# Turning eight tiles in one out-of-place transpose in a fused LoRA kernel

## The chip, the core and the metric

The kernel runs on one core of a Trainium2 chip. The metric is the device time of one execution in microseconds. The kernel before took 124.73 us in the median of three runs (124.68 to 125.21). Engines are named as in the profile: PE is TensorE (matmul), PEld its weight loads, DVE is VectorE, ACT is ScalarE, POOL is GpSimd, SP is SyncE, which here issues all transfers on one queue.

## The reference

A low-rank correction is added to an activation tensor:

```python
batch, seq, d_model, r = 16, 512, 768, 16
lora = np.matmul(np.matmul(x, A), B)      # x: 8192 x 768, A: 768 x 16, B: 16 x 768
return (x + scale * lora).astype(np.float32)   # scale = 0.5
```

All tensors are float32 in memory. x and the output are 25.2 MB each; A and B are 48 KB each.

## The kernel before

The 8,192 rows of x are 64 tiles of 128 rows. They come in five parts of 8, 8, 16, 16 and 16 tiles (`PARTS`), by seven loads: load 0 (2 tiles), load 1 (6), load 2 (8), load 3 (16), load 4 (16), loads 5 and 6 (8 each). `x_sb` has room for 48 tiles; the last 16 take the place of the first 16. SP issues the loads 0 to 4 at the start, then store 0 when group 0 is summed, store 1 when group 1 is summed, load 5 when store 0 has landed, load 6 when store 1 has landed, and then the stores 2 (16 tiles, groups 2 and 3), 3 (16 tiles, groups 4 and 5), 4 and 5 (8 tiles each, groups 6 and 7). The result is added in place, so each store goes out of the same tiles.

The computation works on eight groups of eight tiles (`GROUP`), and each group goes through six steps:

1. **Narrowing** (`narrowed`): four tiles at a time are cast to float16, the first half of a group by ACT, the second by POOL (in group 0 both by ACT). It writes `xh0` or `xh1`.
2. **Turning** (`turned`): DVE transposes blocks of 32 x 32 of the half group in place, with two float16 values read as one float32 value.
3. **Projecting** (`projected`): 24 matmuls of 128 columns per half group, with a block-diagonal form of A (`w_bd`) as weights, sum y = x A into `ps_yt`. This PSUM tile holds both halves.
4. **Spreading**: four ACT instructions (L222) scale y and write it block-diagonally into `y_bd`.
5. **Raising** (`raised`): for each pair of tiles four matmuls with `b_mm` (B, repeated) write y B into one of two PSUM buffers `lora_ps`.
6. **Summing** (`summed`): DVE adds the PSUM buffer to the pair in `x_sb`. There are four pairs in a group.

The order of work on each engine is written out by hand, and semaphores join the engines. DVE does, for each half of a group, the turn of that half of the next group and then the two adds of this group. PE runs a hardware loop over the eight groups. A round raises two pairs of the group before, projects the first half of this group, raises the other two pairs, and projects the second half; the first round raises from a `y_bd` that still holds zeros, and four raises follow the loop. Narrowing a half waits until the projection of that half one group earlier has read the buffer (L175, on `s_y`). ACT narrows the first half of the next group and then spreads this group (L217 to L223). `raised` waits on `s_free` for its PSUM buffer; where a store follows group g, the last of these is given by SP (L137).

At the start POOL builds the weights `w_bd` from A, whose transpose is a DVE instruction at L227, PE repeats B over the partitions by two matmuls (L292), and ACT casts that into `b_mm` (L214).

The two orders in the code:

```python
        for g in range(NG):                 # DVE, L248
            for h in range(2):
                if g + 1 < NG:
                    turned(g + 1, h)
                summed(g, 2 * h)
                summed(g, 2 * h + 1)
```

Of the kernel before, what the change touches and what calls it, by code (L numbers as in the profile page):

```python
# [9 lines left out]
MM_DT = mybir.dt.float16  # L10
# [6 lines left out]
GROUP = 8  # L17

SUB = 4

APART = 8
# [3 lines left out]
def kernel(  # L25
# [25 lines left out]
    def sb(name, shape, dtype):  # L51
        return nc.alloc_sbuf_tensor(name, shape, dtype).ap()
# [15 lines left out]
    pick = sb("pick", [P, NQ, Q], MM_DT)  # L68
    w_bd = sb("w_bd", [P, NC, 2, P], MM_DT)
    b_mm = sb("b_mm", [P, D], MM_DT)  # L70
    xh = [sb(f"xh{h}", [P, SUB, D], MM_DT) for h in range(2)]
    y_bd = sb("y_bd", [P, GROUP, P], MM_DT)
    lora = [ps(f"lora_ps{i}", [P, 2, D]) for i in range(2)]
    y_ps = ps("ps_yt", [P, GROUP, Q])
# [32 lines left out]
    s_a, s_b = sem("s_a"), sem("s_b")  # L107
    s_ready, s_brows, s_pick = sem("s_ready"), sem("s_brows"), sem("s_pick")
    s_w, s_bh, s_bp, s_bm = sem("s_w"), sem("s_bh"), sem("s_bp"), sem("s_bm")
    s_narrow = [sem(f"s_narrow{h}") for h in range(2)]  # L110
    s_y, s_spread = sem("s_y"), sem("s_spread")
    s_turned = [sem(f"s_turned{h}") for h in range(2)]
    s_lora = sem("s_lora")

    s_free = [sem(f"s_free{p}") for p in range(PAIRS)]
    s_sum = sem("s_sum")
# [10 lines left out]
    def on_sync(e):  # L127
        def load(k):
            ld = LOADS[k]
            e.dma_start(out=held(*ld), in_=memory(x2, *ld)).then_inc(s_load[k], 16)  # L130

        def store(k, done):
            st = STORES[k]
            e.wait_ge(s_sum, k + 1)
            if STORED[k] + 1 < NG:

                e.sem_inc(s_free[PAIRS - 1], 1)  # L137
            e.dma_start(out=memory(out2, *st), in_=held(*st)).then_inc(done, 16)

        load(0)  # L140
        load(1)
        e.wait_ge(s_ready, 1)
        e.dma_start(
            out=a_rows[0 : NC * APART : APART, :], in_=A.rearrange("(c e) r -> c (e r)", e=64)
        ).then_inc(s_a, 16)
        e.wait_ge(s_brows, 1)
        e.dma_start(out=b_rows[0 : R * APART : APART, :], in_=B).then_inc(s_b, 16)
        for k in range(2, len(LOADS) - 2):
            load(k)

        e.sem_inc(s_spread, 1)
        for p, n in ((0, 1), (2, 2), (3, 2)):
            e.sem_inc(s_free[p], n)

        e.wait_ge(s_lora, 1)
        e.sem_inc(s_free[1], 1)
        store(0, s_out0)
        store(1, s_out1)
        e.wait_ge(s_out0, 16)
        load(len(LOADS) - 2)  # L160
        e.wait_ge(s_out1, 16)
        load(len(LOADS) - 1)
        for k in range(2, len(STORES)):
            store(k, s_out)

    here = set()

    def narrowed(e, copy, g, h):
        t = g * GROUP + h * SUB
        for k in dict.fromkeys(load_of(t + k) for k in range(SUB)):  # L170
            if (e, k) not in here:
                here.add((e, k))
                e.wait_ge(s_load[k], 16)  # L173
        if g:
            e.wait_ge(s_y, 2 * g + h - 1)  # L175
        n = SUB if (t + SUB - 1) // ROOM == t // ROOM else SUB // 2
        for k in range(0, SUB, n):
            last = copy(out=xh[h][:, ds(k, n), :], in_=tiles(t + k, n))  # L178
        last.then_inc(s_narrow[h], 1)

    def on_gpsimd(e):
        e.memset(a_rows[0 : NC * APART], 0.0).then_inc(s_ready, 1)  # L182
        e.memset(b_rows, 0.0).then_inc(s_brows, 1)  # L183
        e.memset(pick, 0.0).then_inc(s_pick, 1)
        e.memset(w_bd.rearrange("p c k m -> p (c k m)").bitcast(fp32), 0.0)  # L185
        e.memset(y_bd.rearrange("p s m -> p (s m)").bitcast(fp32), 0.0).then_inc(s_ready, 1)  # L186
        e.wait_ge(s_pick, 1)
        e.affine_select(  # L188
            out=pick, in_=pick, compare_op=mybir.AluOpType.not_equal, fill=1.0, base=0,
            pattern=[[0, NQ], [-APART, Q]], channel_multiplier=1,  # L190
        ).then_inc(s_pick, 1)
        e.wait_ge(s_pick, 2)
        e.wait_ge(s_b, 16)
        e.tensor_copy(out=b_half, in_=b_rows).then_inc(s_bh, 1)  # L194
        e.wait_ge(s_ready, 3)
        EACH = Q // APART
        for b in range(NC // EACH):
            e.tensor_copy(  # L198
                out=w_one[:, ds(b * EACH, EACH), :, :],
                in_=a_t[ds(b * Q, Q)].rearrange("i k r (c n) -> i c k r n", n=APART)[..., 0],  # L200
            ).then_inc(s_w, 1)
            e.wait_ge(s_w, b + 1)
        for b in range(NQ):
            e.tensor_copy(  # L204
                out=w_bd[ds(b * Q, Q), :, :, ds(b * Q, R)], in_=w_one
            ).then_inc(s_w, 1)
            e.wait_ge(s_w, NC // EACH + b + 1)
        for g in range(1, NG):
            narrowed(e, e.tensor_copy, g, 1)

    def on_scalar(e):
        narrowed(e, e.copy, 0, 0)
        e.wait_ge(s_bp, 1)
        e.copy(out=b_mm, in_=lora[0][:, 0, :]).then_inc(s_bm, 1)  # L214
        narrowed(e, e.copy, 0, 1)
        for g in range(NG):
            if g + 1 < NG:  # L217
                narrowed(e, e.copy, g + 1, 0)
            e.wait_ge(s_y, 2 * g + 2)
            for b in range(NQ):  # L220
                q = ds(b * Q, Q)
                last = e.mul(out=y_bd[q, :, q], in_=y_ps[q, :, :], mul=sc)  # L222
            last.then_inc(s_spread, 1)  # L223

    def on_vector(e):
        e.wait_ge(s_a, 16)
        e.transpose(  # L227
            out=a_t[0 : NC * APART].rearrange("i k r c -> i (k r) c"),
            in_=a_rows[0 : NC * APART].rearrange("c (i k r) -> c (k r) i", k=2, r=R),
        ).then_inc(s_ready, 1)  # L230

        def turned(g, h):
            e.wait_ge(s_narrow[h], g + 1)
            v = xh[h].bitcast(fp32)
            e.transpose(out=v, in_=v).then_inc(s_turned[h], 1)  # L235

        def summed(g, p):
            xs = tiles(g * GROUP + 2 * p, 2)
            e.wait_ge(s_lora, (g + 1) * PAIRS + p + 1)
            ins = e.tensor_tensor(out=xs, in0=xs, in1=lora[p % 2], op=mybir.AluOpType.add)  # L240
            if p + 1 == PAIRS and g in STORED:
                ins.then_inc(s_sum, 1)
            elif g + 1 < NG or p + 2 < PAIRS:
                ins.then_inc(s_free[p], 1)

        turned(0, 0)
        turned(0, 1)
        for g in range(NG):  # L248
            for h in range(2):
                if g + 1 < NG:  # L250
                    turned(g + 1, h)
                summed(g, 2 * h)
                summed(g, 2 * h + 1)

    def on_tensor(e):


        def projected(h):
            xv = xh[h].rearrange("p s (c j k) -> p s c j k", c=NC, k=2)
            e.wait_ge(s_turned[h], 1)  # L260
            for m in range(MMS):
                c, k = divmod(m, 2)
                mm = e.matmul(  # L263
                    y_ps[:, ds(h * SUB, SUB), :], w_bd[:, c, k, :], xv[:, :, c, :, k],
                    start=(m == 0), stop=(m == MMS - 1),
                )
                if m == 0:
                    mm.then_inc(s_turned[h], -1)
            mm.then_inc(s_y, 1)

        def raised(p):
            if p == 0:
                e.wait_ge(s_spread, 1)
            free = s_free[(p + 2) % PAIRS]
            e.wait_ge(free, 1)
            t = lora[p % 2]
            mms = []
            for k in range(2):
                for n0, w in ((0, 512), (512, 256)) if k == 0 else ((0, 256), (256, 512)):
                    mms.append(e.matmul(  # L280
                        t[:, k, ds(n0, w)], y_bd[:, 2 * p + k, :], b_mm[:, ds(n0, w)],
                        start=True, stop=True,
                    ))
            if p == 0:
                mms[0].then_inc(s_spread, -1)
            mms[1].then_inc(free, -1)
            mms[-1].then_inc(s_lora, 1)

        e.wait_ge(s_pick, 2)
        e.wait_ge(s_bh, 1)  # L290
        for n0, w in ((0, 512), (512, 256)):
            last = e.matmul(  # L292
                lora[0][:, 0, ds(n0, w)], pick.rearrange("p b r -> p (b r)"),
                b_half[:, ds(n0, w)], start=True, stop=True,
            )
        last.then_inc(s_bp, 1)
        e.wait_ge(s_bm, 1)
        with e.Fori(0, NG):
            for h in range(2):
                raised(2 * h)  # L300
                raised(2 * h + 1)
                if h == 0:
                    e.wait_ge(s_w, NC * APART // Q + NQ)
                projected(h)
        for p in range(PAIRS):
            raised(p)

# [43 lines left out]
```

## Time and profile before

The profiled execution took 125.2 us; its span from the first to the last instruction is 123.4 us.

| | busy us | share of the span |
|---|---|---|
| PE (matmul) | 58.3 | 47% |
| DVE | 82.5 | 67% |
| ACT | 38.7 | 31% |
| POOL | 27.3 | 22% |
| DMA queue q1, 16 engines | | 96.1% |

The queue moved 50.43 MB, 25.26 MB read and 25.17 MB written, 409 GB/s over the span. DVE's adds take 54.1 us in 32 instructions, its in-place transposes 28.2 us in 16. The projection's matmuls take 28.2 us (384), the raising matmuls 42.7 us (144, in two shapes); matmuls overlap each other, so these sums are above the busy time. The last add ends at 105.8 us, and the last store is issued then.

How to read it: "busy" is the time in which at least one instruction of the engine runs. A group of instructions is one line of the code, engine, operation and tile; its row gives the busy time, the mean of one instruction in ns, and the idle time ahead of it with what ended it. A DMA issue row gives the median time from the issue to the landing, which includes waiting behind other transfers in the queue. The granted clock is the share of full speed that TensorE's clock was allowed.

### The profile page before, as it was taken

The numbers are of one execution on the slowest core, as the hardware profiler recorded it, in microseconds if no ns is written. First come the engines' busy times: TensorE is split into PE (matmuls) and PEld (weight loads), VectorE is DVE, ScalarE is ACT, GpSimd is POOL, SyncE is SP. The second block draws the span as 40 slices with busy tenths as digits, with TensorE's granted clock in tenths as the row PEclk, the third lists the DMA queues.
The fourth block names the chain that finished last, engine by engine and source line by source line (L and its number), as shares of the span: only waits on it lengthen the run. The fifth ranks groups of instructions, "written<-read, shape, count | busy, mean of one in ns | idle before, by whom it ended". The sixth has DMA issues, their size and how long they took to land.

```text
span 123.4 us, 1313 instructions
## 1 busy us (share of the span) xinstructions
PE 58.3 (47%) x530; PEld 39.2 (32%) x530; DVE 82.5 (67%) x49; ACT 38.7 (31%) x43; POOL 27.3 (22%) x25
## 2 busy tenths in 40 slices
PE   0000249948565994844854775576484452000000
PEld 0000028736352862523614534255253311000000
DVE  0000555059985999999999999999999889200000
ACT  0001992760094085264083072353400400000000
POOL 7500660071035008005203501700800000000000
PEclk9999999999855599999999999999999999555555
DMA  3999996997999898999999999899989989899980
GB/s 66 422 430 372 430 574 287 510 478 335 462 494 398 382 510 358 398 446 430 430 454 390 446 446 502 382 414 478 462 351 478 446 382 446 382 446 414 438 366 8
DMA packets 1928, 50.43 MB, mean 409 GB/s; under 512 B 236, under 2 KB 236, under 8 KB 392
## 3 DMA queue, kind: packets, MB, share of 16 engines
q1 hardware_dynamic: 1928, 50.43, 96.1%
HBM read 25.26 MB, written 25.17 MB: 409 GB/s over the span
## 4 chain that ended last, share of the span: by engine, by line
DVE 54%; PE 13%; DMA 8%; ACT 5%; issue 4%; SPq 0%; ACTq 0%
DVE x_sb L240 38%; DVE xh L235 16%; DMA x_sb<-in_x_dram 8%; PE ps_yt L263 7%; PE lora_ps L280 6%; ACT xh L178 2%; ACT y_bd L222 1%; ACT L178 1%; ACT b_mm L214 1%; SPq L130 0%; SPq L346 0%; SPq L125 0%; ACTq L173 0%
## 5 line engine op out<-in xcount | busy, mean ns | idle before, releaser
L240 DVE TENSOR_TENSOR x_sb<-x_sb,lora_ps 128x1536 f32<-128x1536 f32 x32 | 54.1, 1732 | 3.2 <-PE lora_ps L280 3.2
L280 PE MATMUL lora_ps<-b_mm,y_bd 128*128 128x512 f16 (+1 forms) x144 | 30.6, 352 | 24.2 <-ACT y_bd L222 10.0
L178 ACT CAST xh<-x_sb 128x3072 f16<-128x3072 f32 x9 | 24.8, 2752 | 29.4 <-PE ps_yt L263 22.3
L235 DVE STREAM_TRANSPOSE xh<-xh 128x1536 f32<-128x1536 f32 x16 | 28.2, 1765 | 8.0 <-ACT xh L178 8.0
L263 PE MATMUL ps_yt<-xh,w_bd 128*128 128x128 f16 x384 | 28.2, 235 | 7.5 <-DVE xh L235 7.5
L178 POOL CAST xh<-x_sb 128x3072 f16<-128x3072 f32 x7 | 19.2, 2746 | 52.6 <-PE ps_yt L263 52.6
L263 PEld LDWEIGHTS ps_yt<-xh,w_bd 128*128 128x128 f16 x384 | 26.0, 105 | 12.7 <-issue 12.3
L280 PEld LDWEIGHTS lora_ps<-b_mm,y_bd 128*128 128x128 f16 x144 | 13.1, 103 | 37.7 <-issue 20.9
L222 ACT ACTIVATE y_bd<-ps_yt 32x256 f16<-32x256 f32 x32 | 12.0, 374 | 18.1 <-PE ps_yt L263 17.8
L227 DVE STREAM_TRANSPOSE a_t<-a_rows 96x1024 f32<-96x1024 f32 x1 | 1.9, 1930 | 12.1 <-DMA a_rows<-in_A_dram 12.1
L292 PE MATMUL lora_ps<-b_half,pick 128*128 128x512 f16 (+1 forms) x2 | 0.8, 504 | 13.4 <-POOL b_half L194 13.4
L178 ACT ACT_TABLE_LOAD x1 | 1.3, 1283 | 11.9 <-DMA x_sb<-in_x_dram 11.9
L292 PEld LDWEIGHTS lora_ps<-b_half,pick 128*128 128x128 f16 x2 | 0.1, 103 | 13.4 <-issue 13.4
L194 POOL CAST b_half<-b_rows 128x768 f16<-128x768 f32 x1 | 0.8, 822 | 7.6 <-DMA b_rows<-in_B_dram 7.6
L204 POOL COPY w_bd<-w_one 32x384 f16<-32x384 f16 x4 | 2.0, 500 | 0.2
L198 POOL CAST w_one<-a_t 32x128 f16<-32x128 f32 x3 | 1.2, 390 | 1.0 <-DVE a_t L227 0.8
L185 POOL MEMSET w_bd<- 128x1536 f32 x1 | 1.4, 1378 | 0.0
L182 POOL MEMSET a_rows<- 96x1024 f32 x1 | 0.9, 948 | 0.5 <-SPq L125 0.5
L214 ACT CAST b_mm<-lora_ps 128x768 f16<-128x768 f32 x1 | 0.8, 798 | 0.0
L183 POOL MEMSET b_rows<- 128x768 f32 x1 | 0.7, 734 | 0.0
L186 POOL MEMSET y_bd<- 128x512 f32 x1 | 0.5, 522 | 0.0
L188 POOL TENSOR_SCALAR_AFFINE_SELECT pick<-pick 128x128 f16<-128x128 f16 x1 | 0.3, 306 | 0.0
(5 smaller groups left out, 0.6 us busy)
## 6 DMA issues: line engine op xcount, KB each, us to landing
x_sb<-in_x_dram SPq DMA_DIRECT2D x2, 6144.0 KB, 36.8
out_dram<-x_sb SPq DMA_DIRECT2D x4, 3072.0 KB, 16.5
out_dram<-x_sb SPq DMA_DIRECT2D x2, 6144.0 KB, 22.0
x_sb<-in_x_dram SPq DMA_DIRECT2D x3, 3072.0 KB, 14.7
x_sb<-in_x_dram SPq DMA_DIRECT2D x1, 2304.0 KB, 10.4
x_sb<-in_x_dram SPq DMA_DIRECT2D x1, 768.0 KB, 4.7
a_rows<-in_A_dram SPq DMA_DIRECT2D x1, 48.0 KB
b_rows<-in_B_dram SPq DMA_DIRECT2D x1, 48.0 KB, 9.4
```

The source lines that it names most:

```text
L178: last = copy(out=xh[h][:, ds(k, n), :], in_=tiles(t + k, n))
L182: e.memset(a_rows[0 : NC * APART], 0.0).then_inc(s_ready, 1)
L185: e.memset(w_bd.rearrange("p c k m -> p (c k m)").bitcast(fp32), 0.0)
L198: e.tensor_copy(out=w_one[:, ds(b * EACH, EACH), :, :], in_=a_t[ds(b * Q, Q)].rearrange("i k r (c n) -> i c k r n", n=APART)[..., 0],).the ...
L204: e.tensor_copy(out=w_bd[ds(b * Q, Q), :, :, ds(b * Q, R)], in_=w_one).then_inc(s_w, 1)
L214: e.copy(out=b_mm, in_=lora[0][:, 0, :]).then_inc(s_bm, 1)
L222: last = e.mul(out=y_bd[q, :, q], in_=y_ps[q, :, :], mul=sc)
L227: e.transpose(out=a_t[0 : NC * APART].rearrange("i k r c -> i (k r) c"), in_=a_rows[0 : NC * APART].rearrange("c (i k r) -> c (k r) i", k= ...
L235: e.transpose(out=v, in_=v).then_inc(s_turned[h], 1)
L240: ins = e.tensor_tensor(out=xs, in0=xs, in1=lora[p % 2], op=mybir.AluOpType.add)
L263: mm = e.matmul(y_ps[:, ds(h * SUB, SUB), :], w_bd[:, c, k, :], xv[:, :, c, :, k], start=(m == 0), stop=(m == MMS - 1),)
L280: mms.append(e.matmul(t[:, k, ds(n0, w)], y_bd[:, 2 * p + k, :], b_mm[:, ds(n0, w)], start=True, stop=True,))
```

## The change

The two half-group buffers, turned in place, become two whole-group buffers: `xn` (narrowed) and `xt` (turned). One DVE instruction turns all eight tiles from `xn` into `xt`; only group 0 is turned in two halves. One projection covers eight tiles with 24 matmuls of 256 columns. It is cut in two halves of 12 matmuls around the raising of the last two pairs. The projection of group 0 stands ahead of the loop, and the loop has seven rounds; a round raises group g and projects group g + 1.

The waits change with it. Narrowing waits for `s_taken`, which the second matmul of a projection raises (the turn is over then, so `xn` is free). Turning waits for the whole previous projection (`s_y`), since it overwrites `xt`, and for both narrowed halves. On DVE one turn is followed by four adds. ACT narrows group 0 in three pieces (two, two and four tiles), the first of which needs load 0 only, and makes `b_mm` after that. The semaphore increments that SP made for the loop's empty first round go.

```diff
-    xh = [sb(f"xh{h}", [P, SUB, D], MM_DT) for h in range(2)]
+    xn = sb("xn", [P, GROUP, D], MM_DT)
+    xt = sb("xt", [P, GROUP, D], MM_DT)
...
-        e.sem_inc(s_spread, 1)
-        for p, n in ((0, 1), (2, 2), (3, 2)):
-            e.sem_inc(s_free[p], n)
-
-        e.wait_ge(s_lora, 1)
-        e.sem_inc(s_free[1], 1)
+        for p in range(2, PAIRS):
+            e.sem_inc(s_free[p], 1)
...
-    def narrowed(e, copy, g, h):
-        t = g * GROUP + h * SUB
-        for k in dict.fromkeys(load_of(t + k) for k in range(SUB)):
+    def narrowed(e, copy, g, first, n=SUB):
+        t = g * GROUP + first
+        for k in dict.fromkeys(load_of(t + k) for k in range(n)):
             if (e, k) not in here:
                 here.add((e, k))
                 e.wait_ge(s_load[k], 16)
         if g:
-            e.wait_ge(s_y, 2 * g + h - 1)
-        n = SUB if (t + SUB - 1) // ROOM == t // ROOM else SUB // 2
-        for k in range(0, SUB, n):
-            last = copy(out=xh[h][:, ds(k, n), :], in_=tiles(t + k, n))
-        last.then_inc(s_narrow[h], 1)
+            e.wait_ge(s_taken, g)
+        ins = copy(out=xn[:, ds(first, n), :], in_=tiles(t, n))
+        if g or first:
+            ins.then_inc(s_narrow if g else s_first, 1)
...
     def on_scalar(e):
-        narrowed(e, e.copy, 0, 0)
+        narrowed(e, e.copy, 0, 0, SUB // 2)
+        narrowed(e, e.copy, 0, SUB // 2, SUB // 2)
+        narrowed(e, e.copy, 0, SUB)
         e.wait_ge(s_bp, 1)
         e.copy(out=b_mm, in_=lora[0][:, 0, :]).then_inc(s_bm, 1)
-        narrowed(e, e.copy, 0, 1)
...
-        def turned(g, h):
-            e.wait_ge(s_narrow[h], g + 1)
-            v = xh[h].bitcast(fp32)
-            e.transpose(out=v, in_=v).then_inc(s_turned[h], 1)
+        def turned(first, n):
+            ts = [v[:, ds(first, n), :].bitcast(fp32) for v in (xt, xn)]
+            return e.transpose(out=ts[0], in_=ts[1])
...
-        turned(0, 0)
-        turned(0, 1)
+        for h in range(2):
+            e.wait_ge(s_first, h + 1)
+            ins = turned(h * SUB, SUB)
+        ins.then_inc(s_turned, 1)
         for g in range(NG):
-            for h in range(2):
-                if g + 1 < NG:
-                    turned(g + 1, h)
-                summed(g, 2 * h)
-                summed(g, 2 * h + 1)
+            if g + 1 < NG:
+                e.wait_ge(s_y, g + 1)
+                e.wait_ge(s_narrow, 2 * (g + 1))
+                turned(0, GROUP).then_inc(s_turned, 1)
+            for p in range(PAIRS):
+                summed(g, p)
...
-        def projected(h):
-            xv = xh[h].rearrange("p s (c j k) -> p s c j k", c=NC, k=2)
-            e.wait_ge(s_turned[h], 1)
-            for m in range(MMS):
+        xv = xt.rearrange("p s (c j k) -> p s c j k", c=NC, k=2)
+
+        def projected(first, last):
+            for m in range(first, last):
                 c, k = divmod(m, 2)
                 mm = e.matmul(
-                    y_ps[:, ds(h * SUB, SUB), :], w_bd[:, c, k, :], xv[:, :, c, :, k],
+                    y_ps, w_bd[:, c, k, :], xv[:, :, c, :, k],
                     start=(m == 0), stop=(m == MMS - 1),
                 )
                 if m == 0:
-                    mm.then_inc(s_turned[h], -1)
-            mm.then_inc(s_y, 1)
+                    mm.then_inc(s_turned, -1)
+                if m == 1:
+                    mm.then_inc(s_taken, 1)
+                if m == MMS - 1:
+                    mm.then_inc(s_y, 1)
...
+        e.wait_ge(s_w, NC * APART // Q + NQ)
+        e.wait_ge(s_turned, 1)
+        projected(0, MMS)
         e.wait_ge(s_bm, 1)
-        with e.Fori(0, NG):
-            for h in range(2):
-                raised(2 * h)
-                raised(2 * h + 1)
-                if h == 0:
-                    e.wait_ge(s_w, NC * APART // Q + NQ)
-                projected(h)
+        with e.Fori(0, NG - 1):
+            raised(0)
+            raised(1)
+            e.wait_ge(s_turned, 1)
+            projected(0, MMS // 2)
+            raised(2)
+            raised(3)
+            projected(MMS // 2, MMS)
         for p in range(PAIRS):
             raised(p)
```

## The prediction

> **What bounds the kernel now.** I read the page first: the span, the queue's share, the chain.
>
> ```profile
> span 123.4 us, 1313 instructions
> ...
> DMA  3999996997999898999999999899989989899980
> ...
> q1 hardware_dynamic: 1928, 50.43, 96.1%
> ...
> DVE 54%; PE 13%; DMA 8%; ACT 5%; issue 4%; SPq 0%; ACTq 0%
> ```
>
> The chain blames VectorE, but it ends with the last add; the transfers of the one queue fill 96% of the span, and what is left of it is 1.4 us at the start and some 3 us at the end. So the second thing to read is the stretch after the last add (105.8 us): columns are the busy time of the five engines, the granted clock, the DMA share and GB/s.
>
> ```profile
> 106.00:120.00 14.00, 0.00 (x0) 0.00 (x0) 0.00 (x0) 0.00 (x0) 0.00 (x0) 0.50 0.99 427
> ```
>
> No engine works, and the queue runs 14 us longer at full rate. It is a backlog: the last store is behind others. How far each store was issued before the queue needed it is the spare time of the computation. The DMA answers for one issue at a time (stores 2, 3, 4, 5, and the first load) give the time to landing:
>
> ```profile
> out_dram<-x_sb SPq DMA_DIRECT2D x1, 6144.0 KB, 24.5
> ...
> out_dram<-x_sb SPq DMA_DIRECT2D x1, 6144.0 KB, 19.4
> ...
> out_dram<-x_sb SPq DMA_DIRECT2D x1, 3072.0 KB, 16.7
> ...
> out_dram<-x_sb SPq DMA_DIRECT2D x1, 3072.0 KB, 16.4
> ...
> x_sb<-in_x_dram SPq DMA_DIRECT2D x1, 768.0 KB, 4.7
> ```
>
> By the timeline they were issued at 68.33, 88.27, 98.25 and 105.83, so they landed at 92.8, 107.7, 114.95 and 122.2. Between the last three landings lie 7.28 us for 3,072 KB, so the first load's 768 KB are 1.8 us of data and 2.9 us of fixed latency. A store must therefore be issued 2.9 us before the transfer ahead of it lands, or the queue runs dry. Load 6 (issued 63.07, 14.7 to landing) landed at 77.8. Spare: store 2, 77.8 - 2.9 - 68.33 = 6.5 us; **store 3, 92.8 - 2.9 - 88.27 = 1.6 us**; store 4, 6.5; store 5, 6.2. Stores 0 and 1 (issued 36.38 and 48.38; landed 55.8 and 63.1; load 4 ahead of them 7.28 before 55.8, at 48.5) had 9.2 and 4.5. Store 3 is where a later computation is felt first.
>
> Third, the waits: group 2 cannot begin before its load.
>
> ```profile
> ACT xh L178 <- DMA x_sb<-in_x_dram: 7.1, 1, 7.1
> ```
>
> This wait ends at 33.98 when load 3 lands, whatever the computation does. From there the timeline of one steady group (start, length):
>
> ```profile
> 78.13 1.76 DVE L235 STREAM_TRANSPOSE xh<-xh 128x1536 f32<-128x1536 f32 x1
> ...
> 78.26 1.46 PE L280 MATMUL lora_ps<-b_mm,y_bd 128*128 128x512 f16 x8 [1.67 <-ACT y_bd L222]
> 79.81 3.38 DVE L240 TENSOR_TENSOR x_sb<-x_sb,lora_ps 128x1536 f32<-128x1536 f32 x2
> ...
> 80.03 1.54 PE L263 MATMUL ps_yt<-xh,w_bd 128*128 128x128 f16 x24 [0.32 <-DVE xh L235]
> ...
> 81.58 0.82 PE L280 MATMUL lora_ps<-b_mm,y_bd 128*128 128x512 f16 x4
> 83.12 1.76 DVE L235 STREAM_TRANSPOSE xh<-xh 128x1536 f32<-128x1536 f32 x1
> ```
>
> VectorE has no gap: from start to start 1.68 us for a transpose, 1.65 for an add, 9.97 us for a group (two transposes, four adds).
>
> **The change part by part.**
>
> *Transposes.* Sixteen of 1,536 elements (28.2 us) become two of 1,536 and seven of 3,072. No row shows 3,072 elements, nor a plain out-of-place transpose. The bounds are these:
>
> ```profile
> L178 ACT CAST xh<-x_sb 128x3072 f16<-128x3072 f32 x9 | 24.8, 2752 | 29.4 <-PE ps_yt L263 22.3
> ...
> L227 DVE STREAM_TRANSPOSE a_t<-a_rows 96x1024 f32<-96x1024 f32 x1 | 1.9, 1930 | 12.1 <-DMA a_rows<-in_A_dram 12.1
> ```
>
> Below, 2.75 us, what another engine takes to stream as many elements; above, 3,072 x 1,930/1,024 = 5.79 us, by the only out-of-place transpose, which reads with a stride. I take twice the in-place step, 2 x 1.68 = 3.36: same operation, contiguous as here. A group on VectorE stays at 3.36 + 4 x 1.65 = 9.96 us. The fixed cost saved by merging is inside the lower end, and an earlier add saves nothing as long as the queue is behind.
>
> *Matmuls.* 48 of 128 columns in two bursts of 1.54 us become 24 of 256: as many columns, half the weight loads (105 ns each, already beside the matmuls). I keep 1.54 per half projection at full clock and 2.67 at half clock (the trace has a burst of 2.67 at 33.13). The lower end is half of 1.54, were weight loads alone the limit; the upper end is half clock all through. The lower end changes nothing, since VectorE sets the group; the upper end is the first rival.
>
> *The new waits.* VectorE's transpose now waits for the whole previous projection, with four adds queued behind it. Set the transpose's start at 0: it ends at 3.36; first half projection to 4.9; add 0 to 5.01, raise 2 (0.82) to 5.85; add 1 to 6.66, raise 3 to 7.5; second half to 9.05; adds end 9.96. The projection is 0.9 us early for the next transpose. Then the y_bd copies (4 in 1.53) end at 10.6 and raise 0 at 11.5, wanted at 9.96 + 3.36 = 13.3: 1.8 us early. The casts wait for the second projection matmul (at about 3.6) and take 2.75 on ScalarE and GpSimd side by side, done 6.4, wanted at 9.96. ScalarE's y_bd copies stand behind its cast and are wanted later, at 9.05. Every wait is covered by the adds; if that cover went (half clock), the projection would end at 3.36 + 2.67 + 1.36 + 1.36 + 2.67 = 11.4 and a group would cost 1.5 us more.
>
> *The start.* ScalarE's table load and first cast go ahead of load 1 (first load in at 5.7), the b_mm copy behind the cast of tiles 4 to 7 (16.0 to 16.8). VectorE: A's transpose to 14.03, turns to 15.8 and 17.8. Projection 0 on TensorE ahead of the loop, 2 x 2.67 at half clock: 17.9 to 23.2; the sixteen raises on a still empty y_bd in the first round of the old loop (2.72 and 1.91 us) go. Transpose 1 to 26.6, adds of group 0 to 33.3, so store 0 is issued at about 33.4 against 36.38. On SP only semaphore increments and one wait go, at a point where it waits for s_sum anyway: no transfer changes place in its queue. All of it is hidden behind load 3.
>
> *Group 2 on.* Casts 33.98 to 36.73, transpose 36.77 to 40.13. The y_bd copies of group 1 stand behind the ScalarE cast, as before, and end 38.29. The clock was halved here:
>
> ```profile
> 29.81:33.22 3.41, 1.62 (x11) 0.63 (x9) 3.41 (x3) 0.00 (x0) 0.00 (x0) 1.00 1.04 447
> 33.22:43.46 10.24, 7.65 (x56) 6.03 (x56) 8.43 (x6) 4.25 (x5) 2.75 (x1) 0.50 0.92 398
> ```
>
> With that clock: raises 0 and 1 of group 1 from 38.39 (8 matmuls, 2.72) to 41.1, half projection to 43.75, raise 2 to 44.6, raise 3 to 45.4, second half 46.95; adds 40.13 to 43.45, then 44.65 to 48.0. Store 1 is issued at 48.1 (before: 48.38). Four groups of 9.96 bring store 3 to 48.0 + 39.84 + 0.1 = 87.95 (before: 88.27): spare 89.9 - 87.95 = 1.95 us. If the full clock returns after half 2 only, transpose 3 starts at 49.05, store 3 comes at 89.0: spare 0.9. Last group: transpose 7 to 91.2, first half 92.75, raise 3 to 95.35, second half 96.9, y_bd 98.5, raise 99.4, four adds (6.75) 106.15: store 5 at 106.2 against 112.05, spare 5.8. Loads 5 and 6 (landed 70.4 and 77.8) are wanted by casts at about 71.4 and 81.3.
>
> **Sum.** No store is late: 0 us. The profiled execution stays at 125.2 (span 123.4 and 1.8 around it); it stood 0.47 above the median of the runs, so the forecast is the median, **124.7 us**. Half a per cent (0.6 us) is about what a measurement here can tell from no change; the three runs spread over 0.53.
>
> **The rivals.**
>
> *Half clock, slower.* TensorE's bursts are regrouped, and if the clock is halved in two more of the groups 2 to 5, store 3 comes 3 us later, at 90.95: 1.05 us too late, 125.8 us. All four: 93.95, 128.8. It decides from 1.95 us on. For it: before, the clock fell at 33.2 after a stretch with 1.62 us of matmuls in 3.41. Against: the new group has as many columns in as much time, and at half clock it would run without a gap from 3.36 to 11.4, as it did before from 38.39 until the clock came back at 43.46.
>
> The Trainium skill (TensorE: Matmul & The Clock Gate, "Why this matters for your kernels") says that the clock stays up if no idle gap between bursts exceeds some 3 us; by that rule this rival falls away in groups 3 to 7, whose longest gap is 1.6 us (from 9.05 to 10.65), and store 3 comes at 87.95. The trace does not agree with it: the longest TensorE gap between 17 us and the drop at 33.2 was 1.67 us. So the rival keeps its chance.
>
> *Dear transposes, slower.* At 5.79 each is 2.43 dearer; five lie before store 3: 87.95 + 12.15 = 100.1, 10.2 too late, 135 us. It decides from 0.39 us per transpose (a transpose of 3.75). For it only the strided row.
>
> *Transfers disturbed less, faster.* Store 2 landed 15.0 after load 6, store 3 14.85 after store 2, where 2 x 7.28 = 14.56 is the undisturbed step: 0.73 us lost. If the computation's traffic caused it and the new order doesn't, 124.0. Nothing ties the two together in the trace.
>
> **How the numbers follow.** Forecast (no store late) 0.73; half clock 0.12; dear transposes 0.08; transfers 0.07. Hence faster 0.07, same 0.73, slower 0.20. Range: low 124.0 from the third; high 126.8, the case of two groups at half clock on top of the late clock in group 2 (spare 0.9 instead of 1.95, so 2.1 too late); outside are the dear transposes and the long half clock, some 0.14.
>
> **What would show it.** The queue's share near 96%, its full rate again from the last add to 120; store 3 issued between 87 and 89.9; the 3,072-element transpose at 3.3 to 3.5 us, no VectorE gap from group 3 to 6; store 0 near 33.4. Wrong if store 3 is issued past 90, or if the queue shows a hole.

## The result and the profile after

The changed kernel took 124.35 us in the median of 8 runs (124.30 to 124.49), beside 124.97 us for the kernel before in its 8 runs (124.68 to 125.21). The ratio is 0.9954, with a 95% interval of 0.9940 to 0.9967. By the bound of half a per cent that is no change, but the two sets of runs do not overlap: some 0.6 us were gained here, where the forecast had no gain. Beside the experiments below the kernel before had medians of 124.70 to 124.87, which makes the gain 0.35 to 0.5 us; 0.6 is the upper end.

The profiled execution took 124.31 us. From its page, the span, the busy share of the queue in 40 slices, the queue, and the chain:

```profile
span 122.5 us, 883 instructions
...
DMA  3999997996997997999999999999799799799990
...
q1 hardware_dynamic: 1928, 50.43, 96.6%
...
DVE 49%; DMA 24%; issue 4%; POOL 3%; PE 2%; SPq 2%; POOLq 0%; DVEq 0%
```

The queue is as full as before. After the last add (104.5 us) it goes on at its full rate, with every engine idle:

```profile
106.00:119.00 13.00, 0.00 (x0) 0.00 (x0) 0.00 (x0) 0.00 (x0) 0.00 (x0) 0.50 1.00 431
```

So the bound is where the prediction put it. A steady group of the changed kernel in the timeline (start and length in us):

```profile
66.53 3.36 DVE L229 STREAM_TRANSPOSE xt<-xn 128x3072 f32<-128x3072 f32 x1
...
67.16 1.46 PE L281 MATMUL lora_ps<-b_mm,y_bd 128*128 128x512 f16 x8 [1.67 <-issue]
...
69.81 6.71 DVE L234 TENSOR_TENSOR x_sb<-x_sb,lora_ps 128x1536 f32<-128x1536 f32 x4
...
70.03 1.50 PE L260 MATMUL ps_yt<-xt,w_bd 128*128 128x256 f16 x12 [1.42 <-DVE xt L229]
...
73.91 1.50 PE L260 MATMUL ps_yt<-xt,w_bd 128*128 128x256 f16 x12
75.45 1.53 ACT L217 ACTIVATE y_bd<-ps_yt 32x256 f16<-32x256 f32 x4 [2.19 <-PE ps_yt L260]
```

VectorE has no gap: 3.28 us from the start of the transpose to the first add, 9.92 us from transpose to transpose (66.53 and 76.45), against 9.97 for the two half groups before. The half projections take 1.50 us.

Where did the gain come from, then? The times to landing of the stores 2 to 5, issued at 66.69, 86.53, 96.44 and 104.53:

```profile
out_dram<-x_sb SPq DMA_DIRECT2D x1, 6144.0 KB, 25.6
...
out_dram<-x_sb SPq DMA_DIRECT2D x1, 6144.0 KB, 20.2
...
out_dram<-x_sb SPq DMA_DIRECT2D x1, 3072.0 KB, 17.6
...
out_dram<-x_sb SPq DMA_DIRECT2D x1, 3072.0 KB, 16.8
```

They landed at 92.3, 106.7, 114.0 and 121.3. Load 6 landed at 77.7 as before (77.8). From there the steps are 14.6, 14.4, 7.3 and 7.3 us, where before they were 15.0, 14.9, 7.25 and 7.3. Nearly the whole difference of the spans (123.4 and 122.5) lies in the transfers of the stores 2 and 3: each lasts 0.4 to 0.5 us less, though both were waiting in a full queue.

The packet records of the two traces show which part of the transfer that is. A packet of 48 KB takes 1,817 ns and one of 24 KB 912 ns, over and over. While the stores 0 to 3 are carried and the engines work (50 to 61.5 us and 78 to 106 us), some 22 of about 453 packets are longer by more than 12 ns. They add up to 1,218 ns before and 933 ns after. Followed from the end of one packet to the start of the next, most of this lies on a single one of the 16 DMA engines (1,199 ns and 844 ns there, its smaller lengthenings counted in). A store has landed when its last engine is done. Before, that engine sent its last data at 121.73 us, and the other fifteen had ended by 120.95; after, it ended at 120.78, and the last of the others at 120.95.

The lengthened packets alone don't make up the 0.95 us by which that engine ended earlier. From its last data of load 4 (47.41 us before, 47.07 after) to its end it lost 1.7 us before and 1.1 after against packets of the usual length. So some 0.6 us of the 0.95 is a smaller loss, over half of it in the lengthened packets of the two stretches and the rest in part where the loads change over to the stores (74 to 78 us). The other 0.3 us is where the engine stood when load 4 ended, which differs from engine to engine (47.05 to 48.00 before). These are traces of one execution each; how the gain of the medians divides, they don't show.

### The profile page after: what moved, and what is told of

Same layout as the page of the kernel before. It is cut to its first block, busy times and chain, and to the rows that moved or that the text cites. A ratio compares the mean times of both kernels' runs of the same rounds, so it can differ in the third digit from the quotient of the medians.

```text
span 122.5 us, 883 instructions
## 1 busy us (share of the span) xinstructions
PE 50.7 (41%) x322; PEld 29.9 (24%) x322; DVE 81.8 (67%) x42; ACT 38.9 (32%) x44; POOL 27.3 (22%) x25
## 4 chain that ended last, share of the span: by engine, by line
DVE 49%; DMA 24%; issue 4%; POOL 3%; PE 2%; SPq 2%; POOLq 0%; DVEq 0%
DVE x_sb L234 33%; DMA x_sb<-in_x_dram 24%; DVE xt L229 16%; POOL xn L171 2%; PE lora_ps L281 1%; PE ps_yt L260 1%; POOL a_rows L176 1%; SPq L142 1%; SPq L129 0%; SPq L146 0%; POOLq L351 0%; DVEq L247 0%; SPq L124 0%
## 5 line engine op out<-in xcount | busy, mean ns | idle before, releaser
L281 PE MATMUL lora_ps<-b_mm,y_bd 128*128 128x512 f16 (+1 forms) x128 | 26.1, 339 | 26.5 <-issue 18.8
L171 ACT CAST xn<-x_sb 128x3072 f16<-128x3072 f32 (+1 forms) x10 | 24.9, 2495 | 37.9 <-DMA x_sb<-in_x_dram 20.9
L229 DVE STREAM_TRANSPOSE xt<-xn 128x3072 f32<-128x3072 f32 (+1 forms) x9 | 27.1, 3007 | 9.3 <-POOL xn L171 9.0
L260 PE MATMUL ps_yt<-xt,w_bd 128*128 128x256 f16 x192 | 25.3, 282 | 11.5 <-DVE xt L229 11.5
L171 POOL CAST xn<-x_sb 128x3072 f16<-128x3072 f32 x7 | 19.2, 2748 | 46.4 <-PE ps_yt L260 32.8
L260 PEld LDWEIGHTS ps_yt<-xt,w_bd 128*128 128x128 f16 x192 | 18.7, 100 | 18.9 <-issue 14.6
L281 PEld LDWEIGHTS lora_ps<-b_mm,y_bd 128*128 128x128 f16 x128 | 11.0, 100 | 39.5 <-issue 21.6
## 6 DMA issues: line engine op xcount, KB each, us to landing
x_sb<-in_x_dram SPq DMA_DIRECT2D x2, 6144.0 KB, 36.8
```

What stands on the lines that cost most here:

```text
L171: ins = copy(out=xn[:, ds(first, n), :], in_=tiles(t, n))
L229: return e.transpose(out=ts[0], in_=ts[1])
L260: mm = e.matmul(y_ps, w_bd[:, c, k, :], xv[:, :, c, :, k], start=(m == 0), stop=(m == MMS - 1),)
L281: mms.append(e.matmul(t[:, k, ds(n0, w)], y_bd[:, 2 * p + k, :], b_mm[:, ds(n0, w)], start=True, stop=True,))
```

## The experiments

Three theories of the gain: A, one DMA engine is held up in proportion to the instructions that the core executes (1,313 before, 883 after); B, it comes from the earlier issue of the stores; C, the long out-of-place transpose disturbs the transfers less. Besides, the reading that the queue is the bound, with a spare time in front of store 3, was to be tested for itself. Ratios are to the kernel before, run beside each experiment (its medians were 124.70 to 124.87).

### More matmuls for the same columns

```diff
-                mm = e.matmul(
-                    y_ps, w_bd[:, c, k, :], xv[:, :, c, :, k],
-                    start=(m == 0), stop=(m == MMS - 1),
-                )
+                whole = m in (0, MMS - 1)
+                for s0, n in ((0, GROUP),) if whole else ((0, 4), (4, 4)):
+                    mm = e.matmul(
+                        y_ps[:, ds(s0, n), :], w_bd[:, c, k, :], xv[:, ds(s0, n), c, :, k],
+                        start=(m == 0), stop=(m == MMS - 1),
+                    )
```

> The changed kernel with its projection cut back to 128 columns: the first and the last of the 24 matmuls stay whole, the 22 between are two of 128 columns each, 46 a group. VectorE's and the queue's order stay. Theory A (one of the 16 DMA engines is held up while stores run, in proportion to the instructions that the core executes; 1.70 us with 1313 instructions before, 1.14 us with 883 after, so 1.3 ns each): 352 instructions more, that engine 0.46 us later, and as it ended 0.17 us ahead of the last one, some 0.3 us more: 124.65. Theory B (the earlier issue of the stores made the gain): store 3 is still issued near 86.5, 124.35. Theory C (one long out-of-place transpose disturbs the transfers less): 124.35.

The second form has `((0, 3), (3, 3), (6, 2))` in the place of the two halves.

> The same with three matmuls (96, 96 and 64 columns) in place of each of the 22, 68 a group. The second half projection then ends at 9.5 of 9.96 us by the weight loads (34 of about 58 ns a half), so VectorE should still have no gap. Theory A: 704 instructions more than the changed kernel, that engine 0.92 us later, 0.75 us more: 125.1. Theories B and C: 124.35.

Measured: 125.88 us with 46 matmuls (ratio to before 1.0082, interval 1.0064 to 1.0101) and 126.14 us with 68 (1.0117, 1.0096 to 1.0137). Theories B and C, which said 124.35 for both, don't give this. But A is off as well: the first step costs 1.5 us where 0.3 was expected, and the second 0.3 more. The queues in the trace of the first show why:

```profile
q1 hardware_dynamic: 1928, 50.43, 95.1%
q8 instruction: 1, 0.02, 0.1%
...
x_sb<-in_x_dram SPq DMA_DIRECT2D x2, 6144.0 KB, 37.5
```

There is a transfer that the kernels before and after do not have: one instruction packet of 16 KB, which took 1,069 ns on one DMA engine at 34.6 us (at 30.9 us in the second kernel). The median landing of the two long loads goes from 36.8 to 37.5 us, and that engine then stays behind: it ended its data at 122.9 us, the rest by 121.1. The program of TensorE is 22 matmuls longer in the loop and 22 ahead of it. So there is a second cost beside the one of theory A.

### The transpose in two

```diff
-                turned(0, GROUP).then_inc(s_turned, 1)
+                turned(0, SUB)
+                turned(SUB, SUB).then_inc(s_turned, 1)
```

> The changed kernel with each transpose of 3,072 elements as two of 1,536, still out of place. Theory A: seven instructions more, 124.35. Theory C, if the length is what counts: the gain goes, 124.97; if it is the second buffer: 124.35. Theory B: a group 0.01 us longer, 124.35.

Measured: 124.33 us (0.9965, 0.9952 to 0.9978), the time of the changed kernel (124.35). So the length of the transpose plays no part that could be seen.

### More instructions on GpSimd

```diff
             narrowed(e, e.tensor_copy, g, SUB)
+            for k in range(64):
+                e.memset(idle[:, ds(64 * g + k, 1)], 0.0)
```

> The changed kernel with 64 memsets of one column each on GpSimd after each of its seven casts (448 instructions more; GpSimd is idle for 7 us of a group). Theory A, if instructions of any engine count: that engine 0.58 us later, 0.4 us more, 124.75. If only TensorE's instructions count: 124.35. Theories B and C: 124.35.

Measured: 126.34 us (1.0129, 1.0108 to 1.0150), 2 us more than the changed kernel instead of 0.4. Again the program is longer, and a part of it is fetched during the run:

```profile
q14 instruction: 4, 0.03, 0.1%
```

Four instruction packets of 8 KB, at 25.6, 49.1, 68.7 and 88.0 us, 309 ns each. One engine ended at 122.9 us, the others by 121.0. The time alone can't say whether GpSimd's instructions also count in the sense of A. The lengthened data packets speak for it: 1,253 ns with 1,331 instructions, against 933 with 883.

### Fetching apart from executing

First the split only inside the loop, so that the program is 22 matmuls shorter than in the first experiment:

```diff
-        def projected(first, last):
+        def projected(first, last, parted=True):
...
-                for s0, n in ((0, GROUP),) if whole else ((0, 4), (4, 4)):
+                for s0, n in ((0, GROUP),) if whole else (((0, 4), (4, 4)) if parted else ((0, GROUP),)):
...
-        projected(0, MMS)
+        projected(0, MMS, parted=False)
```

> As the kernel with 46 matmuls a projection, but the projection ahead of the loop stays at 24, so that TensorE's program is shorter by 22 matmuls while 154 more are executed in the seven rounds. That kernel took 125.88, and its trace has an instruction packet of 16 KB at 35.1 us, on one of the 16 DMA engines in the midst of the loads; the kernels before and after have none between 0 and 120 us. Theory A (a program that is too long is fetched during the run, and the fetch delays one DMA engine for good): no such packet, and only the small cost by executed instructions is left, 308 more than in the changed kernel: 124.6. Rival D (executed instructions alone make the time): 308 of the 352, so 125.7.

Measured: 125.30 us (1.0047, 1.0030 to 1.0065). The profiled execution took 124.77 us and has no instruction packet within its span. The spans of all eleven executions (122.8 to 123.3, median 122.9) are 0.35 us above those of the changed kernel (median 122.55) and close to those of the kernel before (123.0 beside this run), as theory A has it, and far from what rival D would need (a span of 123.9). But the other executions took about 2.4 us around the span (2.2 to 2.5, one 3.4), where the profiled one took 2.0 and the changed kernel takes 1.8. What that half microsecond outside the span is stays open, so the total is neither theory's number.

Then the other way round, the same executed matmuls from a longer program:

```diff
-        with e.Fori(0, NG - 1):
+        for _ in range(NG - 1):
             raised(0)
```

> The changed kernel with TensorE's loop written out: the same 322 matmuls are executed, from a program of 322 in place of 82. Theory A: instruction packets during the run, each delaying one DMA engine by 1 us or more; several, so 125.5 to 127. Rival D: as the changed kernel or a little below it, 124.3.

Measured: 125.96 us (1.0096, 1.0080 to 1.0111), with 869 executed instructions.

```profile
q8 instruction: 2, 0.03, 0.1%
```

Two instruction packets of 16 KB, at 43.8 and 75.6 us. The execution count hardly changed and the time rose by 1.6 us: rival D is out, and the cost of a program that has to be fetched is shown. The other pair agrees: with the split in the loop alone the spans had a median of 122.9 us, with the split ahead of the loop as well, and a fetch, 124.1. The lengthened packets add up to 813 ns, in keeping with 869 instructions.

### The gain without the change

```diff
                 c, k = divmod(m, 2)
+                if k:
+                    continue
                 mm = e.matmul(
                     y_ps[:, ds(h * SUB, SUB), :], w_bd[:, c, k, :], xv[:, :, c, :, k],
-                    start=(m == 0), stop=(m == MMS - 1),
+                    start=(m == 0), stop=(m == MMS - 2),
                 )
```

> The kernel before with every second projection matmul left out (192 in place of 384; the odd columns of x are not projected, so the sum is incomplete). Order, waits, in-place transposes of half groups and store times stay as before; VectorE sets the group there. Theory A: 929 instructions in place of 1313, one DMA engine delayed 0.5 us less: 124.4, the time of the changed kernel. Theory B (earlier stores) and C (the transposes): 124.9, the time before.

Measured: 124.34 us (0.9969, 0.9956 to 0.9982). This kernel keeps the in-place transposes of half groups, leaves out half of the projection and has 929 instructions, and it takes the time of the changed kernel. Its store 3 is issued between those of the two (88.27 and 86.53), its store 5 as in the changed kernel (104.53):

```profile
87.60 0.34 SPq L138 DMA_DIRECT2D out_dram<-x_sb  x1
...
104.47 0.33 SPq L138 DMA_DIRECT2D out_dram<-x_sb  x1
```

Theory C is out, since the transposes are the old ones. For B the stores 3 and 5 are earlier than before here too (0.7 and 1.4 us), so B is left to the next experiment.

### The spare time of store 3

```diff
+                e.transpose(out=spare[:, ds(0, 1), :].bitcast(fp32), in_=xn[:, ds(0, 1), :].bitcast(fp32))
                 turned(0, GROUP).then_inc(s_turned, 1)
```

> The changed kernel with one transpose of one tile (384 elements, about 0.45 us) into a spare buffer ahead of each of the seven long ones on VectorE. In its trace store 2 landed at 92.3 and store 3 was issued at 86.53, so store 3 had 92.3 - 2.9 - 86.5 = 2.9 us to spare. Transfers as the bound: five delays, 2.3 us, less than the spare: 124.35. Computation as the bound: 3.1 us more, 127.5.

Measured: 124.43 us (0.9967, 0.9956 to 0.9978). Store 3 is issued 2.1 us later than in the changed kernel, and later than in the kernel before:

```profile
88.61 0.34 SPq L138 DMA_DIRECT2D out_dram<-x_sb  x1
...
out_dram<-x_sb SPq DMA_DIRECT2D x1, 6144.0 KB, 18.1
```

It landed at 106.7, as in the changed kernel. So a store issued later than before still has the gain, and theory B is out too. With four tiles in place of one:

> The same with four tiles (1,536 elements, 1.68 us). Transfers as the bound with 2.9 us to spare: five delays are 8.4 us, store 3 is 5.5 us late, 129.9, and the queue shows a hole of about that length ahead of store 3. Computation as the bound: seven delays, 11.8 us, 136.1. No bound by either before store 3 (a spare above 8.4): 124.35.

Measured: 130.03 us (1.0427, 1.0409 to 1.0446), where 129.9 was worked out. The windows (busy time of the five engines, granted clock, DMA share, GB/s) show the hole ahead of store 3, which was issued at 96.00:

```profile
88.00:90.00 2.00, 0.73 (x7) 0.66 (x8) 2.00 (x2) 0.25 (x1) 0.20 (x1) 1.00 0.91 393
90.00:92.00 2.00, 2.00 (x11) 1.10 (x9) 2.00 (x2) 2.00 (x1) 2.00 (x1) 0.55 0.00 0
92.00:94.00 2.00, 1.97 (x9) 0.86 (x8) 1.94 (x2) 0.51 (x1) 0.55 (x1) 0.59 0.00 0
94.00:96.00 2.00, 1.19 (x11) 0.77 (x9) 2.00 (x3) 0.75 (x3) 0.00 (x0) 1.00 0.00 0
96.00:98.00 2.00, 1.14 (x8) 0.71 (x8) 2.00 (x2) 0.75 (x2) 0.00 (x0) 1.00 0.93 393
```

No packet starts from 90 to 96 (a window counts a packet where it starts): the last data of store 2 ended at 91.4, and the first of store 3 started at 96.8. Store 2 had landed at 91.9. Store 3, issued into the empty queue, took this long:

```profile
out_dram<-x_sb SPq DMA_DIRECT2D x1, 6144.0 KB, 16.0
```

Of 16.0 us, 14.5 are data (the step between landings in the full queue), so the fixed part that a late store shows is 1.5 us and not 2.9. Store 3 was 96.0 + 1.5 - 91.9 = 5.6 us late, and the kernel took 5.7 us more. The expected 5.5 came from two errors that cancelled: the delay was 9.5 us and not 8.4, and the spare was 92.3 - 1.5 - 86.5 = 4.3 us and not 2.9. So the delay within the spare cost nothing, and of the longer one, what went beyond it came out whole at the end.

### The transfers alone

The code of ScalarE, VectorE and TensorE is taken out, and the stores wait for the loads:

```diff
-            e.wait_ge(s_sum, k + 1)
-            if STORED[k] + 1 < NG:
-
-                e.sem_inc(s_free[PAIRS - 1], 1)
+            for n in ((0, 1), (2,), (3,), (4,), (5,), (6,))[k]:
+                e.wait_ge(s_load[n], 16)
```

> The loads and stores alone, in the same order on the same queue, with no computation (the stores wait for the loads only; the low-rank sum is left out). If the transfers bound both kernels, this takes within 0.6 us of the changed kernel: 123.9 to 124.3, the more so as its latest DMA engine was not the delayed one. If the computation bounds the changed kernel after all, it is well below, under 123.

Measured: 123.88 us (0.9926, 0.9903 to 0.9948; 123.60 to 124.53). By the medians, all the computation of the changed kernel costs less than half a microsecond on top of its transfers. With 69 instructions, none of 452 packets in the two stretches is lengthened by more than 12 ns. But lengthened packets are not all that sets the end: the profiled execution was the longest of the six (124.53), and there one engine ended at 121.13 us, later than any in the trace of the changed kernel, after it had lost 0.45 us between 75 and 78 us, where the loads change over to the stores. Such a loss varies from execution to execution.

### A short loop on GpSimd

```diff
             narrowed(e, e.tensor_copy, g, SUB)
+            if g > 1:
+                with e.Fori(0, 12):
+                    for k in range(4):
+                        e.memset(idle[:, ds(4 * g + k, 1)], 0.0).then_inc(s_idle, 1)
+                    e.wait_ge(s_idle, 4)
+                    e.sem_inc(s_idle, -4)
```

> The changed kernel with a short hardware loop on GpSimd after its casts of groups 2 to 7: twelve rounds of four memsets of one column, a wait and a decrement, some 570 executed instructions more from about 50 in the program, so that no program is long enough to be fetched during the run. Theory A (the held-up DMA engine pays about 1.3 ns for each executed instruction, of any engine): it ends 0.75 us later, 0.55 us more in all, 124.9. If only TensorE's instructions or its matmuls count: 124.35. If an instruction packet appears in the trace all the same, the time says nothing on this.

Measured: 125.73 us (1.0064, 1.0046 to 1.0081), and one instruction packet of 8 KB at 75.6 us. With a fetch in it, the time says nothing on the count of instructions. The lengthenings have the largest sum of all: 1,505 ns with 1,393 instructions.

### Fewer instructions still

```diff
                 c, k = divmod(m, 2)
+                if 1 < m < MMS - 1:
+                    continue
                 mm = e.matmul(
```

> The changed kernel with 21 of the 24 matmuls of each projection left out (the first two and the last stay, so most of x is not projected and the sum is incomplete). All other instructions and waits stay. 547 instructions in place of 883. Theory A: the held-up DMA engine ends 0.44 us earlier, but then another is the last; between the changed kernel and the transfers alone (123.88), some 124.1. If the number of instructions played no part in what the changed kernel gained: 124.35 as before, since the queue is the bound and the adds keep their times.

Measured: 124.03 us (0.9938, 0.9925 to 0.9952), 0.3 us below the changed kernel, where 124.1 was worked out. (By the ratios to the kernel before, 0.9938 and 0.9954, it is 0.2 us.)

```profile
span 122.1 us, 547 instructions
...
PE 44.3 (36%) x154; PEld 16.4 (13%) x154; DVE 81.8 (67%) x42; ACT 38.8 (32%) x44; POOL 27.3 (22%) x25
```

VectorE's busy time is that of the changed kernel (81.8 us); only TensorE executes less. The sums of the lengthened packets, taken as above, for all kernels but the one with the hole, whose transfers lie at other times:

```
executed      lengthening   what
instructions  ns
   69            0          transfers alone
  547          360          21 of 24 projection matmuls left out
  869          813          loop written out
  883          933          the changed kernel
  890          682          transposes in two
  890          839          transpose of one tile added
  929          926          before, half the projection
 1191         1212          46 matmuls, in the loop only
 1235         1213          46 matmuls
 1313         1218          the kernel before
 1331         1253          448 memsets on GpSimd
 1393         1505          short loop on GpSimd
 1587         1435          68 matmuls
```

From 547 instructions on, that is 0.65 to 1.1 ns for each executed instruction, whichever of the two engines had more of them. Kernels with nearly equal counts (883 and 890) differ by up to 250 ns, so the sum is no exact measure of the count. That fewer instructions also shorten the time was shown for TensorE's alone; with more on GpSimd the time has a fetch in it each time. What lengthens the packets stays open: the traces hold no packet for it. It may even be the writing of the profiler's own records, and no run here could tell.

## Why the prediction was right, and where it was not

**The bound** was read rightly. The backlog after the last add, the spare times and the place where a delay is felt first (store 3) hold: a delay of store 3 by 2.1 us cost nothing, and one by 9.5 us cost 5.7 us against the changed kernel. The fixed latency in it was mis-sized: 2.9 us, taken from the first load, where a store into an empty queue showed 1.5. Store 3 had 92.8 - 1.5 - 88.27 = 3.0 us before, not 1.6.

**The transposes.** Taken at 3.36 us between bounds of 2.75 and 5.79, they step in 3.28:

```profile
L229 DVE STREAM_TRANSPOSE xt<-xn 128x3072 f32<-128x3072 f32 (+1 forms) x9 | 27.1, 3007 | 9.3 <-POOL xn L171 9.0
```

The strided row was no guide, and the second buffer costs nothing. The group is 9.92 us for the 9.96 worked out.

**The new waits** are covered, as worked out. In the steady groups VectorE waits for neither the projection nor the raises. Its only wait for the raises is before the last group's adds:

```profile
DVE x_sb L234 <- PE lora_ps L281: 1.4, 1, 1.4
```

**The start and group 2** were a little too slow in the working. Store 0 was issued at 32.39 (33.4 forecast); the projection ahead of the loop took 4.15 us instead of 5.3. In group 2 the half clock ended sooner:

```profile
33.22:40.60 7.38, 2.31 (x8) 1.19 (x9) 3.84 (x2) 4.25 (x5) 2.75 (x1) 0.58 0.99 426
40.60:53.70 13.10, 8.78 (x59) 5.26 (x58) 13.10 (x8) 7.00 (x6) 5.50 (x2) 0.98 0.95 409
```

So store 1 came at 46.87 (48.1), store 3 at 86.53 (87.95) and store 5 at 104.53 (106.2). None of it moved the end.

**The half-clock rival** did not come about. From 41 us to the last matmuls the granted clock is full. When the clock fell, at 34.4, TensorE had stood idle for 3.2 us, and from 41 us on its longest gap was 1.7 us. By the Trainium skill (TensorE: Matmul & The Clock Gate, "Why this matters for your kernels") that is what the clock should do, and this trace agrees with it, as that of the kernel before did not.

**The sum** is the step that failed: "No store is late: 0 us" left out a term. The gain belongs to the third rival, transfers disturbed less, which was priced at 0.73 us and given 0.07. Its price was of the right size (0.9 in the span of the profiled executions, 0.35 to 0.6 in the medians), and "Nothing ties the two together in the trace" was wrong. Most of the loss sat on one of 16 DMA engines, and the count of instructions, 1,313 on the first line of the page, was what the change reduced by 430. The transposes and the store times, which the prediction worked out with care, have no share in it that a run here shows. The number came close to the forecast because the missed term is small, half a per cent at most.

## What to carry to other kernels

Where the queue is full until the end and each engine only has to be early enough, work out the spare time of each store: a change within it cost and gained nothing here on its own account. What then still moved the time was seen on the DMA engines: executed instructions went with longer packets, about 1 ns for each, and the kernels with a longer program, of which 8 to 32 KB were fetched in the middle of the transfers, took 1.4 to 2 us more than the changed kernel. So count the instructions, executed and in the program, before splitting work into smaller pieces or writing out a loop in a kernel that is bound by its transfers.

## What the hardware showed that was not expected

A transfer on 16 DMA engines ends with the slowest of them, and while the queue was full, what one engine lost was not made up: the engine that fetched 16 KB of instructions at 34.6 us was still behind at the end, 122.9 us against 121.1. The delayed kernel with the hole from 91.4 to 96.8 us is the counterpart: there the waiting evened the engines out, and all 16 ended within 0.2 us (126.06 to 126.22).

The Trainium skill (Runtime: NRT & Kernel Launch, "Instruction fetch mechanics") says that instructions are refilled in blocks of 16 KiB and that the cost of crossing such a block is "mostly hidden". The size agrees with the packets of 16 KB on TensorE's queue here; GpSimd's were of 8 KB. The cost does not agree in these kernels: 1.6 us for two fetches when the loop was written out, since they stand in line with the data on the same engines.
